# A decoder block whose instruction order is planned: PSUM rings, row sums by array halves, squares added in pairs, and a search in the planner

## The chip, the cores and the metric

The kernel runs on one core of one Trainium2 chip. A core has five engines, each with its own instruction queue: TensorE (PE in the profile: matrix products from SBUF into PSUM, with weight loads listed apart as PEld), VectorE (DVE), ScalarE (ACT), GpSimd (POOL) and SyncE (SP, which here issues all DMA transfers). The metric is the device time of one execution in microseconds, the median of several runs; less is better.

## The reference

One block over a sequence of 1024 tokens with 1024 features, in float32. What matters here:

```python
h = modulate(rmsnorm(x, norm1_g), shift1, scale1)          # shift, scale, gate from silu(c) @ ada_w + ada_b
u, v, val, gate = split(h @ w_in + b_in)                   # four times 512 features
v = layernorm(gelu(v))                                     # per token
mixed = einsum('hts,bcshd->bcthd', tril(w_s), chunks(v)) + b_s   # chunks of 128 tokens, 8 heads
y_a = rmsnorm(gelu(u) * mixed)
y_b = rmsnorm(silu(groupnorm(causal_conv31(val * sigmoid(gate)))))
x = x + gate1 * (concat(y_a, y_b) @ w_out)
h2 = modulate(rmsnorm(x, norm2_g), shift2, scale2)
x = x + gate2 * ((silu(h2 @ w_g) * (h2 @ w_up)) @ w_ffn_out)     # 2816 hidden features
out = modulate(rmsnorm(x, norm_f_g), shift_f, scale_f)
```

The layernorm's bias passes through the spatial product as that bias times the row sums of `tril(w_s)`.

## The kernel before

Features lie on the 128 partitions and tokens along the free dimension; the tokens are worked in two halves of 512. Each large product is made of three products of rounded parts (`mm3`, lines 747 to 749: high by high, low by high, high by low), where ScalarE makes the high part and VectorE or GpSimd the low one (`weights`, line 731, and `modulated`, line 765). The dense layers at the end use a seven-product scheme for 2 x 2 blocks (`product`, line 1109).

**Order of the work.** First the norm of half 0 (`rstd`) and the products `p` for the conv branch of half 0, which fill all eight PSUM banks and take the feature tiles one after another as weights arrive (lines 879 to 911). Then `u_proj(0)` (tiles `pu`), the norm of half 1 (`r1b`, line 1138), its features `h1_1`, `u_proj(1)`, `spatial_bias`, `v_proj`, the convs, the spatial products (`pm`, line 989), the output projection `w_out` (tiles `po`), and products of the feed-forward layer that are made ahead (`ahead_quad`, tiles `ah`). From about 439 us on come the rest of the feed-forward layer (banks A, B, C) and the final norm.

**PSUM.** Eight banks of 128 x 512 float32 in four rings: mm (3), cv (2), gn (2), nrm (1). A tile takes the bank of its ring that comes free first, in the order of the program. At the start, `warm_bank` (dummy products that keep TensorE active, line 685) and `ada0_bank` (the first modulation column, line 879) stand in mm; line 867 puts the eight accumulators `p0_0, p0_1, p1_0, ...` into cv, cv, gn, gn, mm, mm, mm, nrm. `glu` (lines 821 and 823) reads them: ScalarE takes the sigmoid of the gate bank, VectorE multiplies it with the value bank. `u_proj` takes mm banks.

**rstd** (line 775) squares eight feature tiles, adds them up in groups (line 793, on the engine `add_eng`), and for each group makes four products of 32 array columns that sum over the partitions (line 797); then comes a square root on ScalarE, a reciprocal on VectorE, and products that spread the result (line 806). The tuple `groups` says how many squares are added before a pass of products: `(1,) * 8` means eight passes and no addition. The squares lie in a ring of five tiles (`tmp`).

**spatial_bias** (line 847) makes the row sums of the spatial weights on TensorE: two products with a stationary matrix of ones, 128 array columns wide and 512 tokens long (line 850), each with four heads. A head needs only 64 of the rows, so VectorE reads the upper or the lower half of the bank, in eight instructions (line 855).

**The planner.** `fix_order` (line 565) builds a graph of all instructions with a price for each, and fixes each engine's order, SyncE's included. `forward` (line 391) is a list scheduler by rank; `backward` gives each step its distance from the end as a new rank; this is repeated for twelve sets of margins. `replay` (line 494) runs a given order through the model with random lateness added to the steps, and the order with the best mean of eight replays is kept. In the prices, `Clock.tensor` (line 338) charges a change between full and partial use of the array (fewer than 128 rows or columns), and line 142 charges the products of 32 columns. Line 200 draws an edge between two uses of a tile when one of them writes, and also between two readers of a PSUM tile on different engines.

Of the kernel before, what the change touches and what calls it, by code (L numbers as in the profile page):

```python
# [11 lines left out]
ALU = mybir.AluOpType  # L12

P = 128
S = 1024
D = 1024
# [37 lines left out]
def tile_order():  # L54
# [19 lines left out]
           (0.02, 0.03, 0.3), (0.02, 0.05, 0.5), (0.03, 0.02, 0.5), (0.005, 0.1, 0.8), (0.01, 0.0, 1.0),  # L74
           (0.02, 0.1, 0.0), (0.015, 0.05, 0.5))
N_REPLAYS = 8


class Step:
# [52 lines left out]
def duration(s):  # L132

    width = max([o.width for o in s.reads + s.writes] or [0])
    two_in = sum(o.space == "SB" for o in s.reads) >= 2
    if s.engine == "PE":
        n, m = s.writes[0].width, s.reads[1].width
        if not s.reads[0].f32:
            t = (n + 32) / 2400 * (0.5 if m == 64 else 1)
        else:  # L140
            k = s.reads[0].box[1] - s.reads[0].box[0]
            t = max({128: 0.219, 32: 0.068}.get(m, 0.109 if k > 64 else 0.055) * n / 128, 0.2 if n < 32 else 0.0)
        return t, t + 0.176, 0
    if s.engine == "Activation":
        psum = any(o.space == "PSUM" for o in s.reads)
        t = 0.238 + width * 0.0007 if psum else 0.2 + width * 0.00085
        t += 0.00015 * width * sum(o.width == 1 for o in s.reads[1:])
        return (t + 0.1, t + 0.105, 0) if len(s.writes) > 1 else (t - 0.097, t + 0.009, 0)
    if s.engine == "DVE":
        if s.kind in ("Memset", "BNStatsAggregate"):  # L150
            return 0.09, 0.18, 0
        if s.kind == "BNStats":
            return 0.61, 0.7, 0
        if s.kind == "Reciprocal":
            t = 0.153 + width * 0.00623
# [12 lines left out]
        if width <= 8:  # L168
            t = 0.153
        return t - 0.08, t + 0.011, max(t - 0.15, 0.05) if port else 0  # L170
    if s.engine == "Pool":
        if s.kind == "TensorTensor":
            t = 0.21 + width * 0.00211
            return t - 0.04, t + 0.01, t - 0.15
        return (0.1, 0.12, 0) if s.kind == "Memset" else (1.05, 1.1, 0)
    return DMA_ISSUE, DMA_ISSUE, 0


class Graph:


    def __init__(self, instructions, edges, stacked, reusing):
        self.steps = []
        uses, live, tiles, order, bank = {}, {}, {}, {}, {}
        for ins in instructions:
            if not type(ins).__name__.startswith("Inst"):
                continue
            s = Step(ins, len(self.steps))
            for operands, written in ((s.reads, False), (s.writes, True)):
                for o in operands:  # L190
                    if not hasattr(o.tile, "tag"):
                        continue
                    if o.name not in live:
                        live[o.name], uses[o.name], tiles[o.name] = [], [], o.tile
                        if o.tile.tag and o.space != "DRAM":
                            order.setdefault(o.tile.tag, []).append(o.name)
                    kept = []
                    for other, wrote, box in live[o.name]:
                        if other is not s and meet(box, o.box):
                            if written or wrote or (o.space == "PSUM" and other.engine != s.engine):  # L200
                                s.before.add(other.n)
                            if written and covers(o.box, box):
                                continue
# [21 lines left out]
        self.uses = uses  # L225
# [102 lines left out]
class Clock:  # L328
# [9 lines left out]
    def tensor(self, t, s):  # L338

        if s.partial != self.partial:  # L340
            self.partial = s.partial
            t += 0.09 if s.partial else 0.12
        w = int(t / CLOCK_WINDOW)
        slow = 2 if self.throttled and self.active.get(w - 1, 0.0) < CLOCK_WINDOW / 2 else 1
        end = t + slow * s.issue
        a = t
# [144 lines left out]
    return tail  # L491


def replay(g, order, follows, late):

    before = [set(s.before) for s in g.steps]
    for old, new in follows:
        for n in g.first[new]:
            before[n].update(m for m in g.final[old] if m != n)
    done, free, at, begun = [None] * len(g.steps), [0.0] * len(g.steps), {}, [0.0] * len(g.steps)  # L500
    clock, table, place = Clock(True), None, dict.fromkeys(order, 0)

    def arrival(s):
        t = 0.0
        for n in before[s.n]:
            if done[n] is None:
                return None
            p = g.steps[n]
            if (n, s.n) in g.issued:
                t = max(t, begun[n])  # L510
            elif p.engine == s.engine and not p.dma:
                t = max(t, free[n] if p.engine == "PE" else done[n])
            else:
                t = max(t, done[n] + SIGNAL[p.engine])
        return t

    while True:
        best = None
        for e, steps in order.items():
            if place[e] == len(steps):  # L520
                continue
            s = steps[place[e]]
            if s.n not in at:
                t = arrival(s)
                if t is None:
                    continue
                at[s.n] = t
            t = max(clock.free[e], at[s.n])
            if best is None or t < best[0]:
                best = t, e, s  # L530
        if best is None:
            return max(done)
        t, e, s = best
        if s.table not in (None, table):
            table, t = s.table, t + TABLE_LOAD
        begun[s.n] = t
        done[s.n] = clock.run(s, t)[1] + late[s.n]
        if not s.dma:
            clock.free[e] += late[s.n]
        free[s.n] = clock.free[e]  # L540
        place[e] += 1


def lateness(g, seed):
# [17 lines left out]
        s.issue, s.finish, s.port = issue * (1 + k), finish + issue * k, port * (1 + k)  # L562


def fix_order(tc, edges, stacked, reusing, rounds=5):

    g = Graph(list(tc.nc.cur_bb.bb.instructions), edges, stacked, reusing)
# [2 lines left out]
    for engines, pool, wait in MARGINS:  # L570
        stretch(g, engines, pool)
        order, done, follows = forward(g, list(range(len(g.steps))), wait)
        for _ in range(rounds):
# [6 lines left out]
                continue  # L580
            mean = (first + sum(replay(g, order, follows, late) for late in lates[1:])) / N_REPLAYS
            if best is None or mean < best[0]:
                best = mean, order
    for steps in best[1].values():
        for earlier, later in zip(steps, steps[1:]):
            tc.add_manual_dep(later.ins, earlier.ins.name,
                              mybir.DependencyInfo(mybir.DependencyClass.NoSync, mybir.DependencyReason.DATA),
# [4 lines left out]
def block_kernel(ctx: ExitStack, tc: tile.TileContext, xT, c, ada0, ada, cols, vbias, bs, wsp,  # L592
# [79 lines left out]
    for h in range(2):  # L672
# [3 lines left out]
                                ident, start=True, stop=True).ins  # L676
        with issue_after(sqrt_table):
            A.activation(cact[:, hs(h)], cb, AF.Copy)
    warm_bank = mm_bank("warm")

    def keep_warm(count, ins):

# [162 lines left out]
        nc.sync.dma_start(cstt, cst)  # L845

    def spatial_bias():
        for q in range(2):
            rs = mm_bank(f"rs{q}")
            PE.matmul(rs, ones.broadcast_to([P, P]), wt[:, 4 * q:4 * q + 4, :], start=True, stop=True)  # L850
            for hh in range(4):
                hd = 4 * q + hh
                e, hp = hd % 2, hd // 2
                rows = slice(e * 64, (e + 1) * 64)
                V.scalar_tensor_tensor(bst[rows, hp, :], rs[rows, hh * P:(hh + 1) * P],
                                       col("a_ln_b", hp)[rows], bst[rows, hp, :],
                                       op0=ALU.mult, op1=ALU.add)
# [12 lines left out]
    V.scalar_tensor_tensor(gain, bcol(SCALE1, 0, KD), 1.0, colt[:, _OFF["norm1_g"]:_OFF["norm1_g"] + KD],  # L870
# [737 lines left out]
```

## Time and profile before

| | |
|---|---|
| median of three runs | 977.72 us (976.61 to 978.66) |
| the profiled execution | 976.81 us |
| its span, first to last instruction | 975.1 us |
| granted TensorE clock | 0.996 of full |
| HBM read, written | 142.06 MB, 41.16 MB |

In the profile an instruction row gives its start and its length in us, engine, line, operation, tiles (written <- read), the part of the array in use (rows * columns), the size, and how many instructions are merged into the row. An fp32 product appears as two records. In square brackets stands how long the engine was idle before it, and who ended that. Products on TensorE overlap in their pipeline, so the distance between two starts says more than a length.

### The profile page before, as it was taken

How to read it: one execution, taken by the hardware profiler on the slowest of the kernel's cores; microseconds unless marked ns; L12 is line 12 of the kernel's file. 1: busy time of each engine (PE TensorE's matmuls, PEld its weight loads, DVE VectorE, ACT ScalarE, POOL GpSimd, SP SyncE). 2: the span in 40 equal slices, each digit the busy share in tenths (PEclk: the TensorE clock that was granted, in tenths of full speed). 3: DMA queues.
4: the chain of work that ended last, by engine and by line, in shares of the span. 5: the costliest groups of instructions: out<-in, count | busy, mean ns of one | idle time of the engine just before them, and what ended most of it. 6: DMA issues, size and time to landing. Idle time of an engine off the chain costs nothing.

```text
span 975.1 us, 13473 instructions
## 1 busy us (share of the span) xinstructions
PE 959.4 (98%) x4766; PEld 782.4 (80%) x4766; DVE 867.0 (89%) x1206; ACT 472.4 (48%) x752; POOL 397.9 (41%) x240
## 2 busy tenths in 40 slices
PE   8999999999999999999999999999999999999996
PEld 6877777778878778888888888888888888888875
DVE  5999999899999553799999999999989989969956
ACT  5788466643564653465233333333336437227426
POOL 0069888556453312574454535545443100000113
PEclk9999999999999999999999999999999999999998
DMA  8983451434465424864666667777658937415104
GB/s 324 338 304 101 157 168 65 152 130 140 156 215 185 146 84 166 264 233 140 207 222 239 236 239 248 251 238 233 228 196 284 301 121 266 149 33 168 50 1 173
DMA packets 73682, 184.10 MB, mean 189 GB/s; under 512 B 8208, under 2 KB 10512, under 8 KB 73616
## 3 DMA queue, kind: packets, MB, share of 16 engines
q1 hardware_dynamic: 73616, 183.25, 55.5%
q8 instruction: 37, 0.61, 0.3%
q14 instruction: 29, 0.24, 0.1%
HBM read 142.06 MB, written 41.16 MB: 188 GB/s over the span
## 4 chain that ended last, share of the span: by engine, by line
PE 92%; DVE 4%; DMA 2%; ACT 1%; issue 1%; SPq 0%; DVEq 0%; ACTq 0%
PE B L1109 31%; PE C L1109 19%; PE ah L1109 11%; PE A L1109 4%; PE po L747 3%; PE po L748 3%; PE po L749 3%; PE v L747 2%; PE pu L747 2%; PE v L749 2%; PE pu L748 2%; PE v L748 1%; PE pu L749 1%; PE p L747 1%; PE p L748 1%; PE p L749 1%
## 5 line engine op out<-in xcount | busy, mean ns | idle before, releaser
L1109 PE MATMUL B<-h,w_f 128*128 128x512 f32 x816 | 189.8, 389 | 0.0
L1109 PEld LDWEIGHTS B<-h,w_f 128*128 128x128 f32 x816 | 153.2, 188 | 31.8
L1047 DVE SCALAR_TENSOR_TENSOR cv<-ypad,colt,cv 128x512 f32<-128x512 f32 x216 | 146.7, 744 | 0.2
L1109 PE MATMUL B<-fa,w_d 128*128 128x512 f32 x528 | 124.9, 389 | 0.5 <-DVE x L1465 0.5
L1109 PE MATMUL C<-h,w_f 128*128 128x512 f32 x528 | 123.7, 389 | 0.0
L1109 PEld LDWEIGHTS B<-fa,w_d 128*128 128x128 f32 x528 | 98.9, 188 | 21.5 <-DVE x L1465 0.8
L1109 PEld LDWEIGHTS C<-h,w_f 128*128 128x128 f32 x528 | 99.1, 188 | 20.6
L1109 PE MATMUL ah<-h,wh_a 128*128 128x512 f32 x320 | 101.2, 394 | 0.4 <-ACT sg L821 0.4
L1101 ACT ACTIVATE w_f<-raw_f 128x512 fp32r<-128x512 f32 x68 | 42.5, 630 | 96.9 <-PE B L1109 37.5
L1101 ACT ACTIVATE w_d<-raw_d 128x512 fp32r<-128x512 f32 (+1 forms) x72 | 41.8, 593 | 82.3 <-PE B L1109 33.2
L731 POOL TENSOR_TENSOR wl_a<-raw_a,wh_a 128x1024 fp32r<-128x1024 f32 x20 | 49.1, 2454 | 78.1 <-ACT wh_a L730 78.1
L1404 POOL TENSOR_TENSOR sq_nf<-sq_nf,sq_nf 128x512 f32<-128x512 f32 (+1 forms) x7 | 8.5, 1228 | 166.9 <-ACT sq_nf L1383 162.6
L1102 DVE TENSOR_TENSOR w_f<-raw_f,w_f 128x512 fp32r<-128x512 f32 x68 | 73.0, 1084 | 0.5 <-ACT w_f L1101 0.4
L1109 PEld LDWEIGHTS ah<-h,wh_a 128*128 128x128 f32 x320 | 59.8, 188 | 15.2 <-issue 1.9
L1355 POOL TENSOR_TENSOR x<-x,u 128x512 f32<-128x512 f32 x22 | 37.1, 1688 | 70.3 <-DVE u L1354 42.3
L1109 PE MATMUL C<-fa,w_d 128*128 128x512 f32 (+1 forms) x318 | 64.4, 354 | 0.0
L1109 PE MATMUL ah<-h,wl_a 128*128 128x512 f32 x160 | 62.5, 393 | 0.0
L1109 PEld LDWEIGHTS C<-fa,w_d 128*128 128x128 f32 x318 | 52.6, 189 | 8.8 <-issue 0.4
L1465 DVE SCALAR_TENSOR_TENSOR x<-B,cond,x 128x512 f32<-128x512 f32 x48 | 35.8, 747 | 20.4 <-PE B L1109 20.1
L1102 DVE TENSOR_TENSOR fa<-a,fa 128x512 fp32r<-128x512 f32 x77 | 52.8, 730 | 0.0
L1352 POOL TENSOR_TENSOR x<-x,up 128x512 f32<-128x512 f32 x20 | 32.7, 1633 | 42.2 <-ACT x L1351 42.2
L1101 ACT ACTIVATE fa<-a 128x512 fp32r<-128x512 f32 x77 | 46.1, 626 | 7.2 <-DMA a<-acts 4.0
(258 smaller groups left out, 2130.8 us busy)
## 6 DMA issues: line engine op xcount, KB each, us to landing
acts<-x SPq DMA_DIRECT2D x77, 256.0 KB, 3.0
a<-acts SPq DMA_DIRECT2D x77, 256.0 KB, 4.0
raw_f<-wf SPq DMA_DIRECT2D x32, 512.0 KB, 4.1
ada<-ada SPq DMA_DIRECT2D x24, 512.0 KB, 4.2
x<-ada SPq DMA_DIRECT2D x24, 512.0 KB, 4.1
raw_a<-wf SPq DMA_DIRECT2D x20, 512.0 KB, 3.8
ahead<-ahead SPq DMA_DIRECT2D x40, 256.0 KB, 2.6
raw_o<-wo SPq DMA_DIRECT2D x16, 512.0 KB, 3.5
```

The lines of the kernel that those rows point to most:

```text
L731: lo_eng.tensor_tensor(lo, raw, hi.bitcast(F32), op=ALU.subtract)
L747: PE.matmul(acc, shi, mhi, start=start, stop=False)
L748: PE.matmul(acc, slo, mhi, start=False, stop=False)
L749: PE.matmul(acc, shi, mlo, start=False, stop=stop)
L1047: V.scalar_tensor_tensor(accs[j], src, wc, accs[j], op0=ALU.mult, op1=ALU.add)
L1101: A.activation(dst[:, 0, :], src, AF.Copy)
L1102: lo_eng.tensor_tensor(dst[:, 1, :], src, dst[:, 0, :].bitcast(F32), op=ALU.subtract)
L1109: last_mm = PE.matmul(bank[:, cols], s, m[:, cols], start=first and p == 0 and i == 0, stop=p == n - 1 and i == 2, skip_group_check=True)
L1352: G.tensor_tensor(g0, g0, up0, op=ALU.mult)
L1355: G.tensor_tensor(g1, g1, u2, op=ALU.mult)
L1404: G.tensor_tensor(run, run, t, op=ALU.add)
L1465: V.scalar_tensor_tensor(xs[k][:, part], bank[:, cols], ccol(GATE2, k), xs[k][:, part], op0=ALU.mult, op1=ALU.add)
```

## The change

Four edits in the kernel, and a step added to the planner.

1. `warm_bank` and `ada0_bank` move to the gn ring, and the eight first accumulators are dealt out as mm, mm, mm, cv, cv, gn, gn, nrm.
2. `r1b` adds its squares in pairs: `(2,) * 4`, so GpSimd makes four additions and TensorE four passes instead of eight.
3. `spatial_bias` uses one bank: for each head a product of 64 array columns by 128 tokens, put into the upper or the lower half, and VectorE reads whole rows in four instructions.
4. Prices: a 32-column product of 128 tokens 0.056 us (was 0.068), a change into partial use 0.18 us (0.09), out of it 0.23 us (0.12). Two readers of one PSUM tile on the same engine now also keep their order.
5. After the old planning, `climb` makes up to 300 trials: it takes a stall of TensorE in a replay, walks back along what ended last (data or the queue), raises the rank of the steps on that chain or lowers those that were only ahead in a queue, plans again with `forward`, and keeps the order if the sum over the eight replays is smaller. `replay` is rewritten to be quicker and can give its times back; its rules are the same.

```diff
-            t = max({128: 0.219, 32: 0.068}.get(m, 0.109 if k > 64 else 0.055) * n / 128, 0.2 if n < 32 else 0.0)
+            t = max({128: 0.219, 32: 0.056}.get(m, 0.109 if k > 64 else 0.055) * n / 128, 0.2 if n < 32 else 0.0)
...
-                            if written or wrote or (o.space == "PSUM" and other.engine != s.engine):
+                            if written or wrote or o.space == "PSUM":
...
-            t += 0.09 if s.partial else 0.12
+            t += 0.18 if s.partial else 0.23
...
+def climb(g, lates, mean, order, follows, rank, margins):
...
+        for s in order["PE"]:
+            if begun[s.n] > max(end + 0.05, 5.0):
+                stalls.append((begun[s.n] - end, s.n))
+            end = begun[s.n] + s.issue
...
+    def chain(n, depth):
+
+        found = []
+        for _ in range(depth):
+            ends = [(done[m], m, True) for m in sorted(g.steps[n].before) + waits.get(n, []) if m != n]
+            if n in previous:
+                p = g.steps[previous[n]]
+                ends.append((begun[p.n] + p.issue, p.n, False))
+            if not ends:
+                break
+            _, n, data = max(ends)
+            found.append((n, data))
+        return found
...
+    for _ in range(N_CHANGES):
...
+        n = r.choices([n for _, n in stalls], [t for t, _ in stalls])[0]
+        found = chain(n, r.choice((1, 2, 3, 5, 8, 12, 20)))
+        by, changed = r.choice((0.5, 1.0, 2.0, 4.0, 8.0)), list(rank)
+        if r.random() < 0.5:
+            for m, _ in [(n, True)] + found:
+                changed[m] -= by
+        else:
+            for m, data in found:
+                if not data:
+                    changed[m] += by
...
+        trial = forward(g, changed, wait)
...
+            if sum(ends) < sum(best) - 1e-6:
+                best, order, follows, rank, seen, joined = ends, trial[0], trial[2], changed, {}, None
+    return order
...
-                best = mean, order
-    for steps in best[1].values():
+                best = mean, order, follows, [-t for t in tail], (engines, pool, wait)
+    order = climb(g, lates, *best)
+    for steps in order.values():
...
-    warm_bank = mm_bank("warm")
+    warm_bank = gn_bank("warm")
...
-        for q in range(2):
-            rs = mm_bank(f"rs{q}")
-            PE.matmul(rs, ones.broadcast_to([P, P]), wt[:, 4 * q:4 * q + 4, :], start=True, stop=True)
-            for hh in range(4):
-                hd = 4 * q + hh
-                e, hp = hd % 2, hd // 2
-                rows = slice(e * 64, (e + 1) * 64)
-                V.scalar_tensor_tensor(bst[rows, hp, :], rs[rows, hh * P:(hh + 1) * P],
-                                       col("a_ln_b", hp)[rows], bst[rows, hp, :],
-                                       op0=ALU.mult, op1=ALU.add)
+        rs = mm_bank("rs")
+        for hp in range(4):
+            for e in range(2):
+                PE.matmul(rs[e * 64:(e + 1) * 64, hp * P:(hp + 1) * P], ones.broadcast_to([P, 64]),
+                          wt[:, 2 * hp + e, :], start=True, stop=True)
+        for hp in range(4):
+            V.scalar_tensor_tensor(bst[:, hp, :], rs[:, hp * P:(hp + 1) * P], col("a_ln_b", hp), bst[:, hp, :],
+                                   op0=ALU.mult, op1=ALU.add)
...
-    ada0_bank = mm_bank("ada0")
+    ada0_bank = gn_bank("ada0")
...
-    alloc = [cv_bank] * 2 + [gn_bank] * 2 + [mm_bank] * 3 + [nrm_bank]
+    alloc = [mm_bank] * 3 + [cv_bank] * 2 + [gn_bank] * 2 + [nrm_bank]
...
-        r1b = rstd(x_half(1), D, "n1_1", (1,) * 8, G)
+        r1b = rstd(x_half(1), D, "n1_1", (2,) * 4, G)
```

More of the change, by code (lines that the diff above doesn't have):

```diff
@@ L224, in __init__ @@
                 self.steps[n].after.append(s.n)
-        self.uses = uses
+        self.uses, self.waits = uses, None
         self.tag_of = {name: tag for tag, names in order.items() for name in names}
@@ L491, in backward, with replay @@
     return tail
-def replay(g, order, follows, late):
-    before = [set(s.before) for s in g.steps]
+def replay(g, order, follows, late, times=None):
+    if g.waits is None:
+        g.waits = []
+        for s in g.steps:
+            links = []
+            for n in s.before:
+                p = g.steps[n]
+                if (n, s.n) in g.issued:
+                    links.append((n, 0, 0.0))
+                elif p.engine == s.engine and not p.dma:
+                    links.append((n, 1 if p.engine == "PE" else 2, 0.0))
+                else:
+                    links.append((n, 2, SIGNAL[p.engine]))
+            g.waits.append(links)
+    more = {}
@@ L497, in replay @@
     for old, new in follows:
         for n in g.first[new]:
[L499 to L503, printed above, removed]
+            links = more.setdefault(n, [])
+            for m in g.final[old]:
+                if m != n:
+                    p = g.steps[m]
+                    if p.engine == g.steps[n].engine and not p.dma:
+                        links.append((m, 1 if p.engine == "PE" else 2, 0.0))
+                    else:
+                        links.append((m, 2, SIGNAL[p.engine]))
@@ L504, in arrival @@
+    count = len(g.steps)
+    begun, free, done = [None] * count, [None] * count, [None] * count
+    values = begun, free, done
+    waits, run, steps = g.waits, None, g.steps
+    clock, table = Clock(True), None
+    run, engine_free = clock.run, clock.free
+    queues = [(e, iter(ss)) for e, ss in order.items()]
+    heads = [[e, it, next(it, None), None] for e, it in queues]
+    heads = [h for h in heads if h[2] is not None]
+    def arrival(n):
         t = 0.0
-        for n in before[s.n]:
-            if done[n] is None:
-                return None
[L508 to L514, printed above, removed]
@@ L515, in arrival @@
-        return t
[L517 to L524, printed above, removed]
+        for m, kind, signal in waits[n]:
+            v = values[kind][m]
+            if v is None:
+                return None
+            v += signal
+            if v > t:
+                t = v
+        if n in more:
+            for m, kind, signal in more[n]:
+                v = values[kind][m]
+                if v is None:
+                    return None
+                v += signal
+                if v > t:
+                    t = v
@@ L525, in replay @@
+        return t
+    while heads:
+        best, at = None, 0.0
+        for h in heads:
+            t = h[3]
+            if t is None:
+                t = h[3] = arrival(h[2].n)
                 if t is None:
                     continue
[L527 to L533, printed above, removed]
+            f = engine_free[h[0]]
+            if f > t:
+                t = f
+            if best is None or t < at:
+                best, at = h, t
+        e, it, s, _ = best
+        t = at
@@ L534, in replay @@
         if s.table not in (None, table):
             table, t = s.table, t + TABLE_LOAD
-        begun[s.n] = t
-        done[s.n] = clock.run(s, t)[1] + late[s.n]
+        n = s.n
+        begun[n] = t
+        done[n] = run(s, t)[1] + late[n]
         if not s.dma:
-            clock.free[e] += late[s.n]
-        free[s.n] = clock.free[e]
-        place[e] += 1
+            engine_free[e] += late[n]
+        free[n] = engine_free[e]
+        best[2], best[3] = next(it, None), None
+        if best[2] is None:
+            heads.remove(best)
@@ L544, in lateness @@
+    if times is not None:
+        times[:] = begun, done
+    return max(done)
 def lateness(g, seed):
@@ L562, in stretch, with waiting, links @@
         s.issue, s.finish, s.port = issue * (1 + k), finish + issue * k, port * (1 + k)
+def climb(g, lates, mean, order, follows, rank, margins):
+    import random
+    r = random.Random(1)
+    engines, pool, wait = margins
+    def waiting(late):
+        times, stalls, end = [], [], 0.0
+        replay(g, order, follows, late, times)
+        begun, done = times
+        for s in order["PE"]:
+            if begun[s.n] > max(end + 0.05, 5.0):
+                stalls.append((begun[s.n] - end, s.n))
+            end = begun[s.n] + s.issue
+        return begun, done, stalls
+    def links():
+        previous, waits = {}, {}
+        for steps in order.values():
+            previous.update((b.n, a.n) for a, b in zip(steps, steps[1:]))
+        for old, new in follows:
+            for m in g.first[new]:
+                waits.setdefault(m, []).extend(g.final[old])
+        return previous, waits
+    def chain(n, depth):
[10 more added lines that the diff above has]
+        return found
+    best = [replay(g, order, follows, late) for late in lates]
+    seen, joined = {}, None
+    for _ in range(N_CHANGES):
+        i = r.randrange(len(lates))
+        if i not in seen:
+            seen[i] = waiting(lates[i])
+        begun, done, stalls = seen[i]
+        previous, waits = joined = joined or links()
+        n = r.choices([n for _, n in stalls], [t for t, _ in stalls])[0]
[4 more added lines that the diff above has]
+                changed[m] -= by
+        else:
+            for m, data in found:
+                if not data:
+                    changed[m] += by
+        stretch(g, engines, pool)
+        trial = forward(g, changed, wait)
+        stretch(g, 0.0, 0.0)
+        ends = []
+        for i, late in enumerate(lates):
+            ends.append(replay(g, trial[0], trial[2], late))
+            if sum(ends) > sum(best[:i + 1]) + (1.0 if i < 2 else 2.0):
+                break
+        else:
+            if sum(ends) < sum(best) - 1e-6:
+                best, order, follows, rank, seen, joined = ends, trial[0], trial[2], changed, {}, None
+    return order
@@ L582, in fix_order @@
             if best is None or mean < best[0]:
-                best = mean, order
-    for steps in best[1].values():
+                best = mean, order, follows, [-t for t in tail], (engines, pool, wait)
+    order = climb(g, lates, *best)
+    for steps in order.values():
         for earlier, later in zip(steps, steps[1:]):
```

1 line of the change is left out of this document (added).

## The prediction

> **What bounds the kernel now.** I read the page first, for shares.
>
> ```profile
> span 975.1 us, 13473 instructions
> PE 959.4 (98%) x4766; PEld 782.4 (80%) x4766; DVE 867.0 (89%) x1206; ACT 472.4 (48%) x752; POOL 397.9 (41%) x240
> ```
>
> TensorE is occupied for 98% of the span, VectorE for 89%. Whether VectorE is a second bound cannot be read from an average, so I asked for the busy time by stage (columns: stretch, its length, busy us and instructions of PE, weight loads, DVE, ACT, POOL, then granted clock, DMA share, GB/s).
>
> ```profile
> 61.30:318.00 256.70, 255.51 (x1379) 203.19 (x1379) 249.28 (x374) 151.62 (x220) 170.87 (x92) 1.00 0.46 157
> 318.00:356.00 38.00, 38.00 (x239) 28.16 (x238) 17.00 (x21) 22.60 (x32) 11.71 (x8) 1.00 0.36 128
> 439.00:944.00 505.00, 505.00 (x2229) 417.77 (x2227) 471.08 (x643) 199.15 (x340) 159.67 (x101) 1.00 0.58 195
> 944.00:975.10 31.10, 21.70 (x214) 19.09 (x213) 19.03 (x39) 18.23 (x41) 9.49 (x11) 0.88 0.37 135
> ```
>
> Three things stand here. From 439 to 944 TensorE has no idle time: no new order can gain there, it can only lose. From 61 to 318 both TensorE and VectorE are nearly full (255.5 and 249.3 of 256.7), so work taken from TensorE there is only worth its price if VectorE's chain does not become the next bound. The last 31 us hold 9.4 us of TensorE idleness. Then the waits of TensorE (total, times, longest).
>
> ```profile
> PE c L675 <- ACT cvec L667: 2.8, 1, 2.8
> PE ssq_nf L1413 <- DVE rt_nf L1411: 1.9, 1, 1.9
> PE po L747 <- ACT y_b L1005: 1.1, 1, 1.1
> PE pu L747 <- ACT sg L821: 0.8, 1, 0.8
> PE B L1109 <- DVE x L1465: 0.5, 1, 0.5
> PE ah L1109 <- ACT sg L821: 0.4, 1, 0.4
> ```
>
> The first is the head (the condition vector has to arrive), the second the closing norm. The other four, 2.8 us, are all that another order could remove as waits between those two. The rest of TensorE's loss is hidden in "busy": changes between full and partial array, below.
>
> **First edit, the ring.** The eight first accumulators `p` close within a few products of each other; the next product, `pu`, needs an mm bank. Before, mm holds accumulators five to seven.
>
> ```profile
> 60.72 0.39 PE L748 MATMUL p<-h,wl_k 128*128 128x512 f32 x1
> 60.94 0.39 PE L749 MATMUL p<-h,wh_k 128*128 128x512 f32 x1
> 62.15 0.50 PE L747 MATMUL pu<-h,wh_u 128*128 128x512 f32 x1 [0.82 <-ACT sg L821]
> ```
>
> ```profile
> 58.96 1.28 ACT L821 ACT_TABLE_LOAD   x1
> 60.26 2.42 ACT L821 ACTIVATE sg<-p,colt 128x512 f32<-128x512 f32 x4
> ```
>
> (Start, length, both in us.) Products are issued 0.22 to 0.23 us apart, though one lasts 0.39, since they overlap; `pu` starts 1.21 us after its predecessor, so 0.98 us are lost. Four sigmoids take 2.42 us, 0.6 each: the third gate, an mm bank, is read until 62.07, and `pu` starts at 62.15. With the first three accumulators in mm, the first gate's bank is free at 60.26 + 0.6 = 60.9, ahead of the 61.17 at which `pu` could follow. Gain 0.98 us; zero if the sigmoids slip by over a microsecond in the new order. What is late next is the second mm bank, read by VectorE's product, but TensorE wants it only after the 24 products of one `pu` (5.4 us). The warm-up and ada0 banks move from mm to gn; in both versions two later accumulators take those banks, and TensorE itself writes the warm-up, so I cost that at nothing; were ada0's reader late, the first eight products would wait for it, a few tenths.
>
> **Second edit, squares in pairs.** r1b's eight passes over the squares become four. TensorE's rows of before:
>
> ```profile
> 75.30 0.64 PE L797 MATMUL ssq_n<-sq_n,ones 128*32 128x128 f32 x16
> 75.87 0.50 PE L747 MATMUL pu<-h,wh_u 128*128 128x512 f32 x1
> 76.30 1.64 PE L797 MATMUL ssq_n<-sq_n,ones 128*32 128x128 f32 x48
> 77.87 0.50 PE L748 MATMUL pu<-h,wl_u 128*128 128x512 f32 x1
> ```
>
> An fp32 product is two records, so a pass of four products is eight. Sixteen records take 75.87 - 75.30 = 0.57 us, forty-eight 77.87 - 76.30 = 1.57: 0.25 a pass, and four passes fewer save 1.0 us. The number of breaks into `pu` (two here) may go to one or three, 0.4 either way. In return GpSimd gets four additions:
>
> ```profile
> L793 POOL TENSOR_TENSOR sq_n<-sq_n,sq_n x5: 1281/1289/1295, 228.7 to 250.5; 128x512 f32<-128x512 f32 x5
> ```
>
> 4 x 1.29 = 5.2 us. Each waits for two ScalarE squares; queued behind it on GpSimd are the `wl_u` parts, the conv taps' sums and then the low halves of h1_1, which `pu` of half 1 needs. What hides them:
>
> ```profile
> 62.55 1.69 ACT L789 ACTIVATE sq_n<-x 128x512 f32<-128x512 f32 x3
> ```
>
> ```profile
> 65.62 1.31 POOL L1042 TENSOR_TENSOR s<-s,cp 128x512 f32<-128x512 f32 x1 [4.21 <-ACT cp L1041]
> ```
>
> Three squares are there by 64.2, eleven us ahead of the first pass, and GpSimd is idle for 4.2 us until 65.6. I cost the additions at nothing; without that cover they cost up to 5.2 us (the slow rival).
>
> **Third edit, row sums by halves.** Two full products of 512 columns become eight of 64 array columns by 128.
>
> ```profile
> 109.46 1.88 PE L850 MATMUL rs<-wt,ones 128*128 128x512 f32 x4
> 111.12 0.49 PE L747 MATMUL v<-wh_v,h 128*128 128x512 f32 x1
> ```
>
> ```profile
> 155.14 0.39 PE L748 MATMUL v<-wh_v,h 128*128 128x512 f32 x1
> 155.46 1.09 PE L989 MATMUL pm<-wt,vn 128*64 128x128 f32 x16
> 156.48 0.50 PE L749 MATMUL v<-wl_v,h 128*128 128x512 f32 x1
> 156.91 1.09 PE L989 MATMUL pm<-wt,vn 128*64 128x128 f32 x16
> 157.94 0.50 PE L747 MATMUL v<-wh_v,h 128*128 128x512 f32 x1
> ```
>
> Now: 111.12 - 109.46 = 1.66 us. Then: the same eight products as a `pm` run, 156.48 - 155.46 = 1.02, and its entry, 155.46 - 155.14 = 0.32 instead of 0.23, so 1.11. Gain 0.55 us; about 0.9 if the run stands beside another partial one, 0.1 if the search breaks it in two. The Trainium skill's TensorEngine Tiling has two rules that pull apart here: up to twofold speed for a dimension of at most 64 (Theoretical Speedup), and a drain of TensorE at every change of tiling mode (Key Properties). By the first alone the gain would be 0.83 us; the two runs quoted show the drain's price, so the 0.55 stays. On VectorE the eight updates of `bst` become four:
>
> ```profile
> L855 DVE SCALAR_TENSOR_TENSOR bst<-rs,colt,bst x8: 332/350/358, 113.6 to 118.1; 64x128 f32<-64x128 f32 x8
> ```
>
> At 0.35 us each, and twice the rows at the same 128 columns taken as the same time, 1.4 us of VectorE go (none, if a row cost as much as a column).
>
> **Fourth edit, planner and search.** This is the unknown. The planner's prices move towards these rows: it charged 0.21 us for entering and leaving a partial run, now 0.41. From the rows above: two `pm` runs with one product between take 157.94 - 155.46 = 2.48 us; the break costs that less two full runs without it, and one run of 32 records shows what those take:
>
> ```profile
> 151.52 1.97 PE L989 MATMUL pm<-wt,vn 128*64 128x128 f32 x32
> 153.41 0.50 PE L747 MATMUL v<-wh_v,h 128*128 128x512 f32 x1
> ```
>
> 1.89 + 0.23 = 2.12, so a break is 0.36 us; the old price was too low. Breaks of this kind, one full product (once two) between partial runs, stand at 75.87 and 156.48 as quoted; with those of the later group norms I count five in the trace, 1.8 us. The search then changes ranks back along the chain of each stall and keeps what shortens the modelled end. Its field is the 2.8 us of four waits less the 0.8 counted above, 1.8 of breaks and 1.9 in the tail: at most 5.7 us. The other end is a loss: every queue is reordered, SP's loads and GpSimd's included, and one new wait as long as the longest of those four (1.1) or two of them cost 1 to 2 us. I take a gain of 1.6, a third or so of the field, nearer to the gain, since the waits it hunts are real rows and the prices it uses now agree with rows. The added order between two readers of one PSUM bank on one engine binds only instructions that run one after another anyway: nothing, or an ACT instruction of 0.6 us put later.
>
> **Sum.** 0.98 + 1.0 + 0.55 + 1.6 = 4.1 us. The profiled execution took 976.81 us (span 975.1 and 1.7 around it), 0.9 under the median of 977.72. From it: 972.7; from the median: 973.6. I name **973.5**. A measurement here tells about 0.2%, 2 us, from no change.
>
> **Rivals.** *The saving is swallowed at y_b.* The 2.5 us of the first three edits are won before 112 us; at 355.6 TensorE waits for y_b, which hangs on VectorE's conv taps. If VectorE is the bound, TensorE merely waits longer. VectorE is idle for 7.4 of 256.7 us up to 318, and hands on at most its own 1.4 us: 977.7 - 1.4 = 976.3, or no gain at all, 977.7. Against it: between the last tap and y_b there is a long stretch,
>
> ```profile
> 317.96 0.75 DVE L1047 SCALAR_TENSOR_TENSOR cv<-ypad,colt,cv 128x512 f32<-128x512 f32 x1
> ```
>
> ```profile
> 355.66 2.06 DVE L1003 SCALAR_TENSOR_TENSOR yn_b<-s,colt,ssq_b 128x512 f32<-128x512 f32 x3 [2.75 <-PE ssq_b L806]
> ```
>
> 37 us, in which VectorE is busy for 17: that is order, not work, and the search walks just this chain. Chance 0.21.
>
> *GpSimd's additions hold VectorE up.* Place: 62 to 80 us. Two rows of one instruction, and GpSimd beside the second:
>
> ```profile
> 56.98 1.21 DVE L703 SCALAR_TENSOR_TENSOR ada<-ada,cact 128x1024 f32<-128x1024 f32 x1
> 59.22 3.28 DVE L703 SCALAR_TENSOR_TENSOR ada<-ada,cact 128x1024 f32<-128x1024 f32 x1 [0.30 <-DMA ada<-ada]
> ```
>
> ```profile
> 59.02 2.39 POOL L731 TENSOR_TENSOR wl_u<-raw_u,wh_u 128x1024 fp32r<-128x1024 f32 x1 [2.52 <-ACT wh_u L730]
> ```
>
> Alone 1.21 us; beside a GpSimd subtraction 3.28, ending 1.1 us after it: it stood still. The Trainium skill's SBUF — State Buffer (Who interferes with whom) says so: a VectorE instruction with two SBUF inputs and a GpSimd one that reads SBUF exclude each other. The trace agrees (3.28 against 1.21). Four additions could so cost VectorE 5.2 us, less 1.4 saved: 3.8. If y_b hands all of it on, 977.7 + 3.8 = 981.5; with half the additions blocking, 977.7 + 1.2 = 978.9. It decides from 1.4 us of blocking on, and only if the 37 us give nothing. Against it: the conv taps, most of VectorE's work there, read one operand from PSUM and take 0.75 us wherever GpSimd is. I name 980; chance 0.12.
>
> *The search takes most of its field.* 4.5 of 5.7: 977.7 - 2.5 - 4.5 = 970.7, and 969.5 with merged passes in the second and third edit. Chance 0.2.
>
> **How the numbers follow.** Forecast (972 to 975.7) 0.47, larger gain 0.2, swallowed 0.21, slower 0.12. Faster by over 0.2%: 0.47 + 0.2 and a little of the swallowed case, 0.68; same 0.2; slower 0.12. The range reaches from the larger gain, 969.5, to the swallowed case's end and a little beyond, 978.3.
>
> **What would show it.** Right: `pu` follows `p` at 0.23 us near 61; r1b's passes are 32 records, not 64, and take about a microsecond less; `rs` is 16 records in about 1.1 us; fewer single products between partial runs; the wait for y_b shorter; 439 to 944 still free of waits. Wrong: h1_1 or y_b waits that grow by what the head saved, VectorE's ada products longer near 62 to 80, a new wait in the 505 us stretch, or a later end of the tail.

## The result, and the profile after

The changed kernel takes 970.45 us (median of four, 969.72 to 971.5) against 977.37 before (976.61 to 978.66): 6.9 us less, a ratio of 0.9929 with an interval of 0.9911 to 0.9946. The time lies in the range that was given; the gain is 1.7 times the 4.1 us of the sum. In the profiled executions the span went from 975.1 to 968.1 us.

The page's first lines after, then the waits of TensorE (total, times, longest). Line numbers have grown: 747 to 749 are now 857 to 859, 797 is 907, 1109 is 1217.

```profile
span 968.1 us, 13436 instructions
PE 955.2 (99%) x4746; PEld 782.0 (81%) x4746; DVE 861.3 (89%) x1202; ACT 473.7 (49%) x752; POOL 402.8 (42%) x244
```

```profile
PE c L785 <- ACT cvec L777: 2.9, 1, 2.9
PE ssq_n L907 <- DVE sq_n L896: 1.1, 3, 0.5
PE ssq_nf L1521 <- DVE rt_nf L1519: 1.0, 1, 1.0
PE ssq_nf L1502 <- POOL sqs_nf L1512: 0.5, 1, 0.5
PE p L1011 <- DVE h L1002: 0.3, 1, 0.3
```

What is left are the head (the first, second and last rows) and the closing norm. The waits for the sigmoid, for y_b, for `ah` and for `x`, 2.8 us together before, are all gone. The stages (stretch, length, busy us and instructions of PE, weight loads, DVE, ACT, POOL, clock, DMA share, GB/s) say the same:

```profile
61.30:318.00 256.70, 256.70 (x1376) 206.08 (x1375) 248.81 (x373) 154.28 (x223) 182.98 (x99) 1.00 0.47 156
318.00:356.00 38.00, 38.00 (x243) 28.91 (x242) 19.95 (x23) 21.71 (x30) 4.93 (x4) 1.00 0.32 110
439.00:944.00 505.00, 505.00 (x2256) 417.69 (x2255) 464.10 (x644) 197.82 (x336) 154.72 (x98) 1.00 0.59 194
```

TensorE is full in all these stretches, and 439 to 944 holds more products than before (2256 against 2229 records), since everything stands earlier.

Where the time came from is read by setting the start of the same product in both timelines side by side (us):

| event on TensorE | before | after | ahead by |
|---|---|---|---|
| first `p` | 17.49 | 17.04 | 0.46 |
| first `pu` | 62.15 | 60.69 | 1.46 |
| first `v` | 111.12 | 107.48 | 3.64 |
| first `po` of half 0 | 211.53 | 207.93 | 3.60 |
| first `po` that reads y_b of half 1 | 357.12 | 350.85 | 6.27 |
| first B of the down projection | 743.32 | 736.99 | 6.33 |
| end of the span | 975.10 | 968.14 | 6.96 |

So 0.5 us in the head, 1.0 at the ring, 2.2 between there and `v` (passes and row sums), nothing for the next hundred us, 2.7 in the stretch that ends with y_b, nothing in 390 us of dense products, 0.6 in the tail.

Most of the 2.7 us can be named. Between the first `po` of half 0 and the `po` that reads y_b of half 1, both traces hold the same products. Before, TensorE waits there for 1.5 us (1.1 for y_b, 0.4 for `ah`), after not at all. The partial products stand in 11 runs before and in 9 after; at the 0.36 us that a break costs, this is 0.7 us. In the whole timeline behind 60 us, one or two full products stand between two partial runs at five places before and at two after, which is the sign "fewer single products between partial runs".

The three local edits, in the timeline of TensorE after (start, length). First `pu` behind `p`:

```profile
60.46 0.39 PE L859 MATMUL p<-h,wh_k 128*128 128x512 f32 x1
60.69 0.39 PE L857 MATMUL pu<-h,wh_u 128*128 128x512 f32 x1
```

0.23 us, no gap. Then r1b's passes, all in one run:

```profile
72.48 0.39 PE L858 MATMUL pu<-h,wl_u 128*128 128x512 f32 x1
72.80 1.08 PE L907 MATMUL ssq_n<-sq_n,ones 128*32 128x128 f32 x32
73.81 0.50 PE L859 MATMUL pu<-h,wh_u 128*128 128x512 f32 x1
```

And the row sums:

```profile
106.14 0.39 PE L859 MATMUL pu<-h,wh_u 128*128 128x512 f32 x1
106.46 1.09 PE L961 MATMUL rs<-wt,ones 128*64 128x128 f32 x16
107.48 0.50 PE L857 MATMUL v<-wh_v,h 128*128 128x512 f32 x1
```

107.48 - 106.46 = 1.02 us with an entry of 0.32: to the hundredth what the `pm` run had.

The gap at the ring would be closed in this trace without the ring, too. ScalarE's sigmoids run earlier than before:

```profile
58.34 1.85 ACT L931 ACTIVATE sg<-p,colt 128x512 f32<-128x512 f32 x3
```

The third gate is read until 60.19, ahead of the `pu` at 60.69, so its bank, an mm bank in the old ring, would be free in time.

GpSimd's additions stand between its other work, from 52.7 us on:

```profile
52.67 2.27 POOL L903 TENSOR_TENSOR sq_n<-sq_n,sq_n 128x512 f32<-128x512 f32 x1
...
60.78 1.30 POOL L903 TENSOR_TENSOR sq_n<-sq_n,sq_n 128x512 f32<-128x512 f32 x1 [3.04 <-ACT sq_n L899]
62.47 1.29 POOL L903 TENSOR_TENSOR sq_n<-sq_n,sq_n 128x512 f32<-128x512 f32 x1 [0.39 <-ACT sq_n L899]
...
70.42 1.30 POOL L903 TENSOR_TENSOR sq_n<-sq_n,sq_n 128x512 f32<-128x512 f32 x1
```

One of them waited out 3.0 us of idle GpSimd and nothing on TensorE waits for them. That leaves the question where the other 3.8 us come from: head, y_b and tail, which no local edit touches.

### The profile page after: what moved, and what is told of

It is laid out like the page before. It is cut to its first block, busy times and chain, and to the rows that moved or that the text cites. A ratio compares the mean times of both kernels' runs of the same rounds, so it can differ in the third digit from the quotient of the medians.

```text
span 968.1 us, 13436 instructions
## 1 busy us (share of the span) xinstructions
PE 955.2 (99%) x4746; PEld 782.0 (81%) x4746; DVE 861.3 (89%) x1202; ACT 473.7 (49%) x752; POOL 402.8 (42%) x244
## 4 chain that ended last, share of the span: by engine, by line
PE 97%; DMA 1%; DVE 1%; SPq 0%; ACT 0%; issue 0%; DVEq 0%; ACTq 0%
PE B L1217 31%; PE C L1217 19%; PE ah L1217 11%; PE A L1217 4%; PE po L858 3%; PE po L857 3%; PE po L859 3%; PE p L859 3%; PE p L857 3%; PE p L858 3%; PE v L857 2%; PE v L859 2%; PE pu L859 2%; PE v L858 2%; PE pu L857 2%; PE pu L858 1%
## 5 line engine op out<-in xcount | busy, mean ns | idle before, releaser
L1210 DVE TENSOR_TENSOR w_f<-raw_f,w_f 128x512 fp32r<-128x512 f32 x68 | 75.5, 1118 | 1.7 <-ACT w_f L1209 1.7
L1460 POOL TENSOR_TENSOR x<-x,up 128x512 f32<-128x512 f32 x20 | 34.9, 1744 | 45.7 <-ACT x L1459 45.7
L1210 DVE TENSOR_TENSOR w_d<-raw_d,w_d 128x512 fp32r<-128x512 f32 (+1 forms) x72 | 48.6, 686 | 0.7 <-ACT w_d L1209 0.6
```

Source lines behind the costliest of these rows:

```text
L1210: lo_eng.tensor_tensor(dst[:, 1, :], src, dst[:, 0, :].bitcast(F32), op=ALU.subtract)
L1460: G.tensor_tensor(g0, g0, up0, op=ALU.mult)
```

## The experiments

Twelve kernels, each compared with the kernel before on the same chip. "A plan" below is what the planner puts out without trials of the search. The kernel before took 977.40, 977.58 and 977.79 us on the three chips used, so kernels are compared with one another by their ratios; a difference of 0.1% between two of them is not clear of noise.

| kernel | median us | ratio to before | interval |
|---|---|---|---|
| edits, old planner (edits_only) | 976.06 | 0.9990 | 0.9982 to 0.9999 |
| old edits, new planner with search (search_only) | 972.57 | 0.9951 | 0.9939 to 0.9964 |
| all but the trials (no_climb) | 972.01 | 0.9947 | 0.9933 to 0.9960 |
| ring alone, order pinned (ring_pinned) | 976.58 | 0.9992 | 0.9983 to 1.0001 |
| edits and new prices only (prices_only) | 972.72 | 0.9955 | 0.9943 to 0.9967 |
| all, old prices (old_prices) | 974.68 | 0.9974 | 0.9964 to 0.9984 |
| no trials, price of a change doubled (high_prices) | 981.20 | 1.0035 | 1.0022 to 1.0048 |
| before, eight extra GpSimd additions (pool_adds) | 978.86 | 1.0018 | 1.0009 to 1.0027 |
| no trials, price of a change a little lower (near_low) | 976.36 | 0.9983 | 0.9974 to 0.9992 |
| no trials, a little higher (near_high) | 974.40 | 0.9966 | 0.9953 to 0.9978 |
| no trials, old 32-column price (switch_only) | 973.77 | 0.9959 | 0.9947 to 0.9972 |
| after with another seed (seed2) | 971.08 | 0.9933 | 0.9921 to 0.9946 |

**The edits without the planner.** The kernel before with the ring, the pairs and the halves.

```diff
-    alloc = [cv_bank] * 2 + [gn_bank] * 2 + [mm_bank] * 3 + [nrm_bank]
+    alloc = [mm_bank] * 3 + [cv_bank] * 2 + [gn_bank] * 2 + [nrm_bank]
...
-        r1b = rstd(x_half(1), D, "n1_1", (1,) * 8, G)
+        r1b = rstd(x_half(1), D, "n1_1", (2,) * 4, G)
...
```

> The kernel before with the ring, the pairs and the halves, planned by the planner of before (no search, old prices). Theory A, each edit carries its local price to the end: 1.1 + 1.5 + 0.55 us off 977.4, so about 974.2, with the wait of po for y_b near 355 still about 1.1 us. Theory B, the saving is swallowed where TensorE waits for y_b: 976.3 to 977.4, with that wait grown to 2 us or more. Either way the orders differ by a planning of their own, which may move the end by a microsecond.

976.06 us: 1.3 us off 977.40, just under theory B's time, but not by its mechanism. The first `v` starts at 108.50, 2.6 us ahead of before, so the three edits pay there as worked out. Then TensorE's waits:

```profile
PE p L747 <- ACT sg L821: 1.2, 1, 1.2
PE po L747 <- ACT y_b L1003: 0.8, 1, 0.8
PE B L1107 <- DVE x L1463: 0.7, 2, 0.5
```

The first row is a new wait near 191 us, where a `vg` product of half 1 waits for a bank that ScalarE still reads; a small new one stands at 819 us. The wait for y_b did not grow, it shrank from 1.1 to 0.8. The plan as a whole, made anew because the graph changed, gave half of the gain back in places of its own.

**The planner without the edits.** New prices, edge and search on the old kernel body (seed 2 for the trials).

```diff
-    alloc = [mm_bank] * 3 + [cv_bank] * 2 + [gn_bank] * 2 + [nrm_bank]
+    alloc = [cv_bank] * 2 + [gn_bank] * 2 + [mm_bank] * 3 + [nrm_bank]
...
-    r = random.Random(1)
+    r = random.Random(2)
```

> The kernel after with the three edits of the kernel proper undone; the new prices, the new edge and the search stay (the search with seed 2 for its random trials). Theory A, the search takes out waits that the order alone made: the four waits of the middle (2.8 us in all) go, also the one of pu for the sigmoid if the search finds a way round it, and the time is 977.4 - 3.8 = 973.6. Theory B, the search needs the freed ring to move anything: 976 to 977.4, with the waits of y_b and of the sigmoid still in the trace.

972.57 us, 4.8 us off: theory A's time, and more; whether the search or the prices did it, this run cannot tell. With the old ring the wait of `pu` for the sigmoid is gone too: `pu` starts at 60.85, 0.22 us behind the last `p`, since the third sigmoid ends at 60.41. One wait of the middle is left:

```profile
PE ah L1219 <- ACT ahead L1234: 0.7, 1, 0.7
```

With the same new planner, the three edits on top are worth about 2 us: 972.57 against 970.45 with them, or by the ratios, with the same seed, 0.9951 against 0.9933 (seed2 below). They do not add up: alone they bring 1.3, the planner alone 4.8, both 6.9.

**All but the trials.**

```diff
-N_CHANGES = 300
+N_CHANGES = 0
```

> The kernel after with no trials of the search: new prices and the new edge only. Theory A, the search itself took the 3.8 us behind the three edits: 970.5 + 3 to 4 = 973.5 to 974.5, with a wait for y_b of about a microsecond back in the trace. Theory C, the new prices did it, since they agree with the trace: 970.5 to 971.5, and no wait over 0.4 us between 61 and 944 us.

972.01 us: theory C's trace, nearly its time. From y_b on TensorE stands where it stands after the full change (350.87 against 350.85, 736.99 against 736.99), and no wait over 0.2 us remains between 61 us and the tail, which begins here with B's wait of 0.5 us at 938.6 (theory C had allowed none over 0.4 before 944):

```profile
PE c L785 <- ACT cvec L777: 3.0, 1, 3.0
PE ssq_nf L1521 <- DVE rt_nf L1519: 1.0, 1, 1.0
PE ssq_nf L1502 <- POOL sqs_nf L1512: 0.6, 1, 0.6
PE B L1217 <- DVE x L1573: 0.5, 1, 0.5
```

So the search did not remove the four waits; the plan from which it set out had none of them. What the trials added is in the tail: the span ends at 968.14 instead of 969.15, and the last row above is missing after. By the medians it is 1.6 us, but the two intervals overlap (0.9911 to 0.9946 and 0.9933 to 0.9960), so the worth of the trials is not shown clear of noise.

**The ring alone, on a pinned order.** Every engine keeps the order of before; only banks change.

```diff
-    alloc = [cv_bank] * 2 + [gn_bank] * 2 + [mm_bank] * 3 + [nrm_bank]
+    alloc = [mm_bank] * 3 + [cv_bank] * 2 + [gn_bank] * 2 + [nrm_bank]
...
+    order = json.loads(zlib.decompress(base64.b85decode("".join(PINNED))))
...
```

> The kernel before, with every engine's order pinned to the one it had, and only the rings changed (warm-up and ada0 in gn, first accumulators mm, mm, mm, cv, cv, gn, gn, nrm). Theory A: pu starts 0.23 us after the last p instead of 1.21, and the end moves by as much: 977.4 - 1.0 = 976.4. Theory B: the same 1.0 us is won near 61 us and given back at y_b, whose wait grows from 1.1 to about 2.1: 977.4.

976.58 us, 0.8 less by the medians, which is theory A's end; the interval just reaches no change. TensorE's rows near 61 us (lines 747 to 749 are 943 to 945 here):

```profile
60.74 0.39 PE L945 MATMUL p<-h,wh_k 128*128 128x512 f32 x1
60.97 0.42 PE L943 MATMUL pu<-h,wh_u 128*128 128x512 f32 x1
```

The gap is closed, as predicted. The first `v` is 0.7 us ahead of before, and so is the `po` that waits for y_b:

```profile
356.42 0.50 PE L943 MATMUL po<-y_b,wh_o 128*128 128x512 f32 x1 [1.10 <-ACT y_b L1201]
```

Its wait is 1.10 us, as before. y_b moved with TensorE, so VectorE is no bound there, and theory B falls at its place. In this trace the lead is lost at another:

```profile
819.71 0.84 PE L1305 MATMUL C<-fa,w_d 128*128 128x512 f32 x3
820.84 0.50 PE L1305 MATMUL B<-fa,w_d 128*128 128x512 f32 x1 [0.28 <-DVE x L1661]
```

A bank of the down projection is read by VectorE until 820.78 here and until 820.69 before: only TensorE came earlier. Ahead of it TensorE leads the trace of before by 0.6 us, behind it by nothing, and the span ends 0.3 us earlier. So a saving in the front can be eaten half a millisecond later, where the old order had no slack. But the medians keep 0.8 us, and single executions differ by more than that, so how much of the ring's microsecond reaches the end of this order stays open.

**Prices, edge, and how far a plan is a draw.** Edits and new prices with the old edge:

```diff
-                            if written or wrote or o.space == "PSUM":
+                            if written or wrote or (o.space == "PSUM" and other.engine != s.engine):
...
-N_CHANGES = 300
+N_CHANGES = 0
```

> The three edits of the kernel proper and the new prices; the old edge, no search. Theory P, the prices are what turned the planning (the version without the search stands at 972.0, the one with none of it at 976.1): 972, with no wait of TensorE over 0.4 us between 61 and 930 us. Theory E, the edge between two readers of one bank did it: 975.5 to 976.5, with the wait for y_b back.

972.72 us, theory P's time: the edge is not needed for most of the gain. Its trace is not quite theory P's, since a wait of 0.7 us stands near 190 us:

```profile
PE ssq_b L907 <- POOL sq_b L903: 0.7, 1, 0.7
```

With the search but the old prices:

```diff
-            t += 0.18 if s.partial else 0.23
+            t += 0.09 if s.partial else 0.12
...
```

> The kernel after with the old prices; the three edits, the new edge and the search of 300 trials stay. Theory P, prices that agree with the chip are what counts, and a search on wrong prices removes waits that are not there: 974 to 976. Theory S, the search finds the waits either way: 971 to 972.5.

974.68 us, in theory P's range. The search left waits in the trace that the change does not have:

```profile
PE p L857 <- ACT sg L931: 1.1, 1, 1.1
PE po L857 <- ACT y_b L1113: 0.6, 1, 0.6
```

What this plan takes without the trials was not measured, and by the runs below it may be one more draw. With the price doubled once more:

```diff
-            t += 0.18 if s.partial else 0.23
+            t += 0.36 if s.partial else 0.46
```

> The kernel after without the search and with the price of a change into and out of partial use doubled once more (0.36 and 0.46 us, some 0.4 us a run more than the trace shows). Theory P: the plan is wrong the other way, waits of TensorE come back, 974 to 976. Theory D, any dearer change keeps the runs together and that is all it needs: 971.5 to 972.5, with fewer partial runs than the 27 of the version without the search. Theory R, each planning is a draw whatever its prices: anywhere from 971 to 977.

981.20 us, slower than before and worse than any theory gave.

```profile
PE p L1011 <- DVE h L1002: 2.4, 1, 2.4
PE ssq_nf L1521 <- DVE rt_nf L1519: 2.3, 2, 1.4
```

The loss is in the head and in the tail. The first `p` starts at 19.35 (17.49 before), since VectorE's `h` comes late. From 19.35 to 27.00 us the granted clock is then 0.62 of full, where before it was 1.00, and the first 24 steps from one `p` to the next take 8.29 us instead of 5.56. No other run here has a clock below 1.00 between 16 and 27 us, and none so long a wait there; whether the wait brought the clock down was not tested. The first `pu` starts at 65.72 (62.15). At the `po` that reads y_b this plan is only 0.8 us behind (357.93 against 357.12), at the end 4.5 (979.62 against 975.10), over half of it lost behind the first B of the down projection. So this run says little on theory P. Two small changes of the price, 0.16 and 0.20 instead of 0.18 and 0.23, then 0.20 and 0.26, were to settle it:

> The three edits, the new edge, no search, and prices of 0.16 and 0.20 us for a change into and out of partial use (0.18 and 0.23 in the version without the search that took 972.0; the trace shows 0.36 us a run in all). Theory P, a price near the chip's gives a good plan: 971.5 to 973. Theory R, each planning is a draw and 972.0 was a lucky one: as likely 974 to 977 as not.

> As near_low with 0.20 and 0.26 us. Theory P: 971.5 to 973.5. Theory R: as likely 974 to 979 as not, with waits between 61 and 944 us in places of their own.

976.36 and 974.40 us. With prices that differ from the change's by 0.02 or 0.03 us, waits are back that no_climb does not have; the first two rows are near_low's, the third near_high's:

```profile
PE p L857 <- ACT sg L931: 1.2, 1, 1.2
PE ah L1217 <- DVE ahead L1234: 0.5, 1, 0.5
```

```profile
PE po L857 <- ACT y_b L1113: 1.1, 1, 1.1
```

And with the new price of a change but 0.068 instead of 0.056 for a 32-column product:

> The three edits, the new edge, no search, the new prices of a change, and the old price of a product of 32 columns (0.068 us for 128 tokens, where the trace shows 0.055 to 0.063). If the price of the change is what counts: 971.5 to 973. If the two prices count together: 974 to 976.

973.77 us, with a wait of its own near 80 us:

```profile
PE ssq_n L916 <- DVE rt_n L913: 1.1, 1, 1.1
```

That speaks for theory R: unsearched plans of almost the same model take 972.0, 972.7, 973.8, 974.4 and 976.4 us. The first three are not told apart by their intervals; the last is clear of the first (0.9974 to 0.9992 against 0.9933 to 0.9960), and its prices of a change, 0.16 and 0.20, add up to just the 0.36 us of the trace. So that the prices agree with the trace is not enough to make a plan good, and the change's plan was a good draw. Whether the new prices make good draws likelier than the old ones is not shown: with the old prices and the edits one unsearched plan was timed, 976.06 us.

**Another seed for the search.**

```diff
-    r = random.Random(1)
+    r = random.Random(2)
```

> The kernel after with seed 2 for the search's random trials. If the search is worth its 1.5 us (972.0 without it, 970.5 with it): 970 to 971, the gain again in the tail behind 930 us, where the version without the search is 1 us behind. If seed 1 was luck: 971.5 to 972.5.

971.08 us, between the two expectations; its interval overlaps that of the change and that of the version without trials. In the middle it has no wait either. Its tail has two that the change does not have:

```profile
PE ssq_nf L1502 <- POOL sq_nf L1512: 0.5, 1, 0.5
PE B L1217 <- DVE x L1573: 0.3, 1, 0.3
```

The second was 0.5 us in the plan that takes 972.0, from which both searches set out; the first is new. The span of this profile is 969.30 us, against 969.15 without any trial, so by the traces this seed gained nothing.

**What GpSimd's additions cost where they don't fit.** The order of before, pinned, with eight additions of 192 columns, whose result nobody uses, behind the third `wl_u`.

```diff
...
+    idle = front.tile([P, 192], F32, name="idle")
+    for _ in range(8):
+        G.tensor_tensor(idle, cact[:, 0:192], cact[:, H:H + 192], op=ALU.add)
```

> The kernel before with every engine's order pinned, and eight additions of 192 columns on GpSimd put behind the third subtraction of wl_u (near 61 us); their result is used by nobody. They take GpSimd about as long as the four additions of the change, 8 x 0.6 = 4.9 us. Theory F, GpSimd's idle time there hides them: 977.4, TensorE's products from 88 us on at the same times. Theory L, they lock VectorE out and the delay is handed on: VectorE's products with ada and cact near 61 to 70 us grow by up to 4.9 us together, the wait for y_b grows, 978.5 to 981.

978.86 us, 1.3 us slower: theory L's lower end, by another way. VectorE's `ada` products beside the additions and right behind them took

```profile
59.24 3.23 DVE L899 SCALAR_TENSOR_TENSOR ada<-ada,cact 128x1024 f32<-128x1024 f32 x1 [0.42 <-DMA ada<-ada]
...
67.67 1.21 DVE L899 SCALAR_TENSOR_TENSOR ada<-ada,cact 128x1024 f32<-128x1024 f32 x1
```

The first is as long as it was (3.28), the second 1.21 us instead of 3.07, since the subtraction that had run beside it came later. No locking out of VectorE was added: the first addition, which began beside the first of these products, took 1.59 us, the others 0.61, so it was GpSimd that waited. Most of the others ran beside VectorE instructions with an operand in PSUM. But ScalarE's rows (start, length, idle before) read:

```profile
74.67 0.72 ACT L1237 ACTIVATE cp<-ypad,colt 128x512 f32<-128x512 f32 x1 [2.45 <-POOL s L1238]
75.30 0.67 ACT L1177 ACTIVATE ya<-pu,colt 128x512 f32<-128x512 f32 x1
76.97 0.72 ACT L1237 ACTIVATE cp<-ypad,colt 128x512 f32<-128x512 f32 x1 [0.99 <-POOL s L1238]
77.59 1.65 ACT L985 ACTIVATE sq_n<-x 128x512 f32<-128x512 f32 x3
```

The conv's scaled taps `cp` have two buffers, which GpSimd frees. GpSimd was late, so ScalarE stood in front of a `cp`, and the squares of r1b, next in its queue, started at 77.6 instead of 75.8. TensorE waited for them, 1.1 us longer than before:

```profile
PE ssq_n L993 <- ACT sq_n L985: 1.3, 2, 1.1
```

## Why the prediction came out as it did

**First edit, right on the old order.** 0.98 us predicted, 1.0 measured (0.46 us ahead at the first `p`, 1.46 at the first `pu`). On the pinned order the gap closed by the bank and the sigmoid that were named. Under the new planner the ring is not what closed it: search_only has the old ring and no gap either.

**Second and third edit, right and 0.6 us short.** 1.0 and 0.55 us predicted, 2.2 together measured. Passes: 2.14 us in two runs before, 1.01 in one run after; the second entry and return went too, which was put down as 0.4 either way. Row sums: exactly the 1.02 us and 0.32 of entry. VectorE's four `bst` updates took 0.342 us each, so the 1.4 us went as well. The additions cost nothing where the new plan put them.

**Fourth edit, the failed step.** "I take a gain of 1.6, a third or so of the field, nearer to the gain, since the waits it hunts are real rows and the prices it uses now agree with rows." By place in the timeline it brought 3.8 us (7.0 less 3.2), more than twice that, and alone, without the edits, 4.8 (search_only); both reasons fell. The search did not take the waits: without it they are gone too (no_climb), and its own part is 1.0 us in the tail of one profile and nothing with another seed. The agreement of the prices is not enough: prices of a change that are nearer to the trace's 0.36 us give 976.4 (near_low). What the runs show in place of the step is a new plan, made before any trial, that has no wait in the middle and fewer breaks. The term should have been written as the difference between two draws of a planner, which in the five plans above lie up to 4.4 us apart, with the waits and breaks in the trace as what a good draw can win.

**The rivals.** *Swallowed at y_b* had its effect right and its place wrong. With the old planner 1.3 of some 2.6 us remain; but the wait for y_b stayed at 1.10 us on the pinned order and shrank in edits_only. In these two traces the gain was lost to a bank read by ScalarE near 191 us and one read by VectorE near 820. *GpSimd holds VectorE up* did not happen: VectorE's six `ada` products between 55 and 85 us took 13.35 us together after the change and 13.27 before. Extra additions cost 1.3 us through ScalarE's queue, not through the lock; eight of them beside VectorE's `ada` products, as the rival had it, were not tried. *The search takes most of its field* gave 970.7, close to the result, and named the waits that went, but not their cause.

**The sum's place in the range.** The forecast's own stretch, 972 to 975.7, missed the result by 1.5 us; the range held it because the larger gain was a case of its own. That the time came out there is in part luck: with prices that add up to just the trace's 0.36 us, the same edits took 976.36 (near_low), outside the forecast's stretch on the other side.

What stays open: why this set of prices and this graph give a plan without waits and their neighbours don't, whether the trials are worth anything beyond noise, and whether they would bring a plan of 976 us down as far as one of 972. None of this was tried far enough to say.

## What to carry to other kernels

Local prices on the engine that is full can be read from the trace: here the ring's and the row sums' came out to a few hundredths of a microsecond, and the passes' fell short only because a break went as well. Whether they reach the end is decided by the order of everything else, and if a planner makes that order anew, its draw can be worth more than the edits (4.8 us here, against about 2): so separate the two with a pinned order or with the planner's change alone, and time several plans before giving a cause. When work is added to an idle engine, look at whose buffers that engine frees and what is queued behind the instruction that waits for them.

## What the runs showed of the hardware

A VectorE instruction of 128 partitions by 128 columns took 0.342 us, one of 64 partitions by 128 columns 0.350 us: the other 64 rows cost nothing. A broken partial run costs TensorE 0.36 us (rows from 151 to 158 us before), and the eight 64-column products of the row sums took the same 1.02 us as those of `pm`, with other operands and another stationary matrix. An addition on GpSimd that began beside VectorE's `ada` product took 1.59 us, the same addition later 0.61 (pool_adds). In one of the fourteen traces (high_prices) the granted clock was 0.62 of full for 7.7 us behind a wait of TensorE of 2.4 us in the head, and 24 steps between products took 2.7 us longer.
